# Spreading the gain row over the partitions ahead of the first expert's products instead of between them

## The chip, the cores and the metric

The kernel runs on one core of a Trainium2 chip. What counts is the device time of one execution in microseconds (us). Three runs of the kernel before gave 1275.82, 1276.06 and 1279.53 us; the median is 1276.06 us.

The engines: PE multiplies matrices (PEld is its load of weights, PEq its sequencer), DVE and ACT work on vectors, POOL is GpSimd, SP only issues transfers (SPq is its queue).

## The reference, cut to what matters

One decoder block over 1024 tokens of width 1024. An adaLN-conditioned branch part (windowed attention and a gated MLP) comes first; then a hierarchical mixture of experts: each token takes one group of four, and two of the eight experts in it.

```python
mod = cs @ w_ada[l] + b_ada[l]
sh1, sc1, g1, sh2, sc2, g2 = [m[:, None, :] for m in jnp.split(mod, 6, axis=-1)]
...
h = rms_norm(x, norm2_g[l]) * (1.0 + sc2) + sh2
x = x + g2 * hierarchical_moe(h, w_router_g[l], ..., w_gate[l], w_up[l], w_down[l])
return rms_norm(x, final_g)
```

For each expert the rows of the tokens that chose it go through `(silu(xb @ w_gate) * (xb @ w_up)) @ w_down`; the result is weighted per token and, in this kernel, scaled by the row `g2` (1024 values, one per column) as it is taken out of PSUM. It is this row `g2` that the change is about.

## The kernel before, in words

The first half of the program (attention, gated MLP, output projection) runs from a list `jobs`; the experts run from a second list `jobs2`. A job has a split (a weight piece in fp32 is split into two parts by ACT, L451, and DVE, L452), products on PE, and hooks: functions that are called once the job's products are written down. `Jobs.run` (L88) goes through the list, so the place of a hook is a place in the order of the program. The program's order is not yet the order on the engines: the tile framework's planner gives each engine its queue. It goes through the instructions with the program's order as priority and takes an instruction when its plan holds its operands to be ready, so a later instruction may be queued ahead of an earlier one that still waits. On the chip each engine then works through its queue strictly in that order. Only inside `tc.manual_schedule` is the written order kept.

The row g2 is worked out during the first half (`later_chunk`, L1086) and stored to a DRAM row, `rowd[3]` (L1125). Between the two halves lies the router: for the last two token tiles the logits are multiplied (`r_logit`, L876), ranks within each expert are counted (`r_rank`, L903 to L906), and the list of tokens per first expert is put together by small products (`tab_tok`, L953 to L955, into one PSUM bank for all tiles) and turned into row numbers on DVE (L958, L938, L939, tile `tok_s`). With them POOL gathers the token rows of the first experts by indirect DMA (`gather`, L1425, fetch on L1416), PE transposes them (`x_t`, L1448), ACT takes the transposes out of PSUM (L1449), and the first expert's products can begin (`side`, L1504; 32 rows per expert, so a 128x128 product per quarter). `order_list` (L1688, first product on L1691) sorts the experts on DVE for all later loads.

The experts' weights stream through the pool `big`, 7 buffers of 2 MB; `Ring` issues the next load from the queue of SP (L1391) when a buffer is given back, which is when its last product or split is done. For unit 0 the jobs 0 to 3 are the gate products (16 instructions each), 4 to 7 the up products.

The row g2 reaches the engines thus: SP loads it to partition 0 of tile `G2` (L1832, 4 KB). `spread` (L1822) then multiplies a column of ones by it, once per half of the row, into one fresh PSUM bank each (L1826; the trace shows each call as two matmuls), and ACT copies each half to all 128 partitions of `G2` (L1827). `in_layout` (L1565, copies on L1569) lays the quarters and halves of the row out for experts with 32 and 64 rows (`G2p[4]`, `G2p[2]`), in six copies on POOL. They are first read when an expert's result is taken out (`y_part`, L1571). All of this hangs on job 2 of `jobs2` (L1833): the program writes it between the third and the fourth gate job of the first expert.

Of the kernel before, what the change touches and what calls it, by code (L numbers as in the profile page):

```python
# [101 lines left out]
def block_kernel(ctx: ExitStack, tc: tile.TileContext, x, c, positions, rel_bias, w_ada, b_ada,  # L102
# [6 lines left out]
    PE, DVE, ACT, POOL, SP = nc.tensor, nc.vector, nc.scalar, nc.gpsimd, nc.sync  # L109

    def f(ap):
        return ap.bitcast(F32)
# [8 lines left out]
    def nm(s):  # L121
        uid[0] += 1
        return f"{s}_{uid[0]}"
# [4 lines left out]
    def bank(shape=(512,)):  # L128
        return psum.tile([P] + list(shape), F32, name=nm("ps"), tag="ps")
# [287 lines left out]
    rowd = [dram.tile([1, D], F32, name=f"rowd{i}") for i in range(4)]  # L417
# [32 lines left out]
    def split_to(hi, lo, src):  # L450
        ACT.copy(hi, src)  # L451
        return DVE.tensor_tensor(lo, src, f(hi), op=OP.subtract)  # L452
# [884 lines left out]
    jobs2 = Jobs(2)  # L1337
# [17 lines left out]
    flat = [c for u in units for c in u]  # L1355
# [47 lines left out]
    def parts(i):  # L1403

        return P // rows_of.get(i, P)

    def x_rows(i):

        q = min(parts(i), 2)
        return q, P if i in range(4) else q * rows_of.get(i, P)  # L1410
# [29 lines left out]
    def x_t(i):  # L1440
        xg = XG.pop(i)
        if parts(i) > 1:
            n = x_rows(i)[1]
            xg = xg[0:n, 0:HT].rearrange("t (p j) -> t j p", j=4)
            xt = f(wk.tile([P, 8, P], F32R, name=nm("xTh"), tag="xTh"))[:, 0:4, 0:n]
            ps = bank((4, P))
            for j in range(4):
                PE.transpose(ps[:, j, 0:n], xg[:, j], ident[0:n, 0:n])  # L1448
            ACT.copy(xt, ps[:, :, 0:n])  # L1449
            XT[i] = xt  # L1450
            return
        xg = xg.rearrange("t (h p j) -> t h j p", h=2, j=4)
        hi = wk.tile([P, 8, P], F32R, name=nm("xTh"), tag="xTh")
        lo = wk.tile([P, 8, P], F32R, name=nm("xTl"), tag="xTl")
        for n in range(2):
            ps = bank((4, P))
            for k in range(4):
                PE.transpose(ps[:, k], xg[:, n, k], ident)
            split_to(hi[:, 4 * n:4 * n + 4], lo[:, 4 * n:4 * n + 4], ps)
        XT[i] = (hi, lo)  # L1460
# [104 lines left out]
    def in_layout(dst, src, q):  # L1565

        n, m = P // q, D // q
        for e in range(q):
            POOL.tensor_copy(dst[n * e:n * e + n], src[n * e:n * e + n, m * e:m * e + m])  # L1569
# [66 lines left out]
    G2 = wk.tile([P, D], F32, name="g2r", bufs=1)  # L1636
    G2p = {q: wk.tile([P, D // q], F32, name=f"g2{q}", bufs=1) for q in (2, 4)}
# [43 lines left out]
    def row(n):  # L1681
        return wk.tile([P, 4, n], F32, name=nm("ol"), bufs=1)

    def fl(ap):
        return ap.rearrange("p a b c -> p (a b c)" if len(ap.shape) == 4 else "p a b -> p (a b)")
    key, cap = row(8), row(8)

    def order_list():  # L1688
        b3_ = wk.tile([P, FE], F32, name=nm("sl"), tag="sl")
        pc_ = bank()  # L1690
        PE.matmul(pc_[:, 0:NE], ones_b, cum[:, 0], start=True, stop=True)  # L1691
        top, rank, sel = row(1), row(1), row(4)
        E, S, at, r8 = (b3_[:, 256 + 32 * k:288 + 32 * k].rearrange("p (a b) -> p a b", a=4) for k in range(4))
        b3 = b3_[:, 0:256].rearrange("p (a b c) -> p a b c", a=4, b=8)
        b4 = wk.tile([P, FE], F32, name=nm("sl"), tag="sl")[:, 0:128].rearrange("p (a b c) -> p a b c", a=4, b=8)
        DVE.scalar_tensor_tensor(fl(key), pc_[:, 0:NE], 32.0, fl(tie), op0=OP.mult, op1=OP.add)
        DVE.tensor_reduce(top, key, axis=AX.X, op=OP.max)

        DVE.tensor_tensor(b3, key.unsqueeze(2).to_broadcast([P, 4, 8, 8]), key.unsqueeze(3).to_broadcast([P, 4, 8, 8]),
                          op=OP.is_gt)  # L1700
        DVE.tensor_reduce(r8, b3, axis=AX.X, op=OP.add)

        DVE.tensor_tensor(sel, fl(top).unsqueeze(1).to_broadcast([P, 4, 4]), top.to_broadcast([P, 4, 4]), op=OP.is_gt)
        DVE.tensor_reduce(rank, sel, axis=AX.X, op=OP.add)
        DVE.tensor_tensor(sel, gid.unsqueeze(2).to_broadcast([P, 4, 4]),
                          fl(rank).unsqueeze(1).to_broadcast([P, 4, 4]), op=OP.is_equal)

        DVE.tensor_tensor(b3, place.unsqueeze(1).unsqueeze(3).to_broadcast([P, 4, 8, 8]),
                          r8.unsqueeze(2).to_broadcast([P, 4, 8, 8]), op=OP.is_equal)
        DVE.tensor_tensor(b3, b3, eid.unsqueeze(2).to_broadcast([P, 4, 8, 8]), op=OP.mult)  # L1710
        DVE.tensor_reduce(S, b3, axis=AX.X, op=OP.add)
        DVE.tensor_tensor(b4, sel.unsqueeze(2).to_broadcast([P, 4, 8, 4]),
                          S.rearrange("p g l -> p l g").unsqueeze(1).to_broadcast([P, 4, 8, 4]), op=OP.mult)
        DVE.tensor_reduce(E, b4, axis=AX.X, op=OP.add)
        oi = ord_i[:, 4:NE].rearrange("p (g r) -> p g r", g=4)
        DVE.tensor_copy(oi, E[0:1, :, 0:7])
        DVE.tensor_scalar(cols[:, 4:NE].rearrange("p (g r) -> p g r", g=4), E[:, :, 0:7], 8.0, None, op0=OP.mult)
        DVE.tensor_copy(cols[:, 0:4], iota_c[:, 0:4])
        for j, (g, r) in enumerate(more):
            DVE.tensor_scalar(cols[:, NE + j:NE + j + 1], E[:, g, r:r + 1], 8.0, 1.0, op0=OP.mult, op1=OP.add)  # L1720

        DVE.tensor_tensor(b4, rank.unsqueeze(3).to_broadcast([P, 4, 8, 4]),
                          gid.unsqueeze(1).unsqueeze(1).to_broadcast([P, 4, 8, 4]), op=OP.is_equal)
        DVE.tensor_tensor(b4, b4, room.rearrange("p g r -> p r g").unsqueeze(1).to_broadcast([P, 4, 8, 4]), op=OP.mult)
        DVE.tensor_reduce(at, b4, axis=AX.X, op=OP.add)
        DVE.tensor_tensor(b3, place.unsqueeze(1).unsqueeze(1).to_broadcast([P, 4, 8, 8]),
                          r8.unsqueeze(3).to_broadcast([P, 4, 8, 8]), op=OP.is_equal)
        DVE.tensor_tensor(b3, b3, at.unsqueeze(2).to_broadcast([P, 4, 8, 8]), op=OP.mult)
        DVE.tensor_reduce(cap, b3, axis=AX.X, op=OP.add)
        for g, n in zip(FIRST, FIRST_ROWS):  # L1730
            if n < P:
                DVE.memset(cap[:, g, 0:1], float(n))
# [83 lines left out]
            DVE.tensor_tensor(tm, tok, blk[:, 2 * k], op=OP.mult)  # L1816
            DVE.tensor_tensor(rows_i[:, k], tm, blk[:, 3], op=OP.add)

    order_list()
    x_t(flat[0])  # L1820

    def spread(dst):  # L1822

        for n in range(2):
            sl, ps = slice(512 * n, 512 * n + 512), bank()
            PE.matmul(ps, ones[0:1, :], dst[0:1, sl], start=True, stop=True)  # L1826
            ACT.copy(dst[:, sl], ps)  # L1827
    low = wk.tile([P, 2], F32, name="low", bufs=1)
    R["low"] = low
    DVE.tensor_scalar(low[:, 0:1], prow, 63.5, None, op0=OP.is_lt)  # L1830
    DVE.tensor_scalar(low[:, 1:2], prow, 31.5, None, op0=OP.is_lt)
    SP.dma_start(G2[0:1], rowd[3])  # L1832
    jobs2.hook(2, lambda: (spread(G2), in_layout(G2p[4], G2, 4), in_layout(G2p[2], G2, 2)))  # L1833
    jobs2.hook(3, combine_weights)
    jobs2.hook(4, visits)
    nj = len(jobs2.jobs)
# [79 lines left out]
    jobs2.hook(f_at, f_load)  # L1916
    jobs2.hook(nj - 30, f_gain)
    jobs2.hook(nj - 20, lambda: (spread(F["g"]), in_layout(F[4], F["g"], 4), in_layout(F[2], F["g"], 2)))
    jobs2.hook(nj - 1, final)
    jobs2.run()  # L1920
# [95 lines left out]
def build(inputs):  # L2016
    import concourse.bacc as _bacc

    nc = _bacc.Bacc("TRN2", target_bir_lowering=False, num_devices=1)
    arrays, args = {}, []  # L2020
    for name in _INS:
        a = np.ascontiguousarray(inputs[name])
        arrays[f"in_{name}_dram"] = a
        args.append(nc.dram_tensor(f"in_{name}_dram", a.shape, mybir.dt.from_np(a.dtype), kind="ExternalInput").ap())
    for i, (shape, dtype) in enumerate(_OUTS):
        dt = mybir.dt.from_np(np.dtype(dtype))
        args.append(nc.dram_tensor(f"out_{i}_dram", shape, dt, kind="ExternalOutput").ap())
    with tile.TileContext(nc) as tc:
        block_kernel(tc, *args)
    return nc, arrays  # L2030
# [8 lines left out]
```

## Time and profile before

| | us |
|---|---|
| median of three runs | 1276.06 |
| the profiled execution | 1274.85 |
| its span, first to last instruction | 1273.2 |
| PE busy | 1147.2 (90%) |
| DVE busy | 772.3 (61%) |
| ACT busy | 555.3 (44%) |
| POOL busy | 221.0 (17%) |
| mean DMA rate | 263 GB/s |

All times below are us from the start of the span of that one profiled execution. A row of the timeline gives the start, the length, engine, line, operation, the tile written and those read, shapes, the number of merged instructions, and in brackets how long the engine had been idle and what released it. [...] The first half ends, and the experts begin, at about 690 us.

### The profile page before, as it was taken

Reading aid. Unit: us, or ns where it says so; the run is one execution under the profiler, and the core shown is the slowest. Engines: PE = TensorE matmul, PEld = TensorE weight load, DVE = VectorE, ACT = ScalarE, POOL = GpSimd, SP = SyncE. Lnnn points to the kernel's source line nnn. Section 1 sums busy time; section 2 is a strip of 40 time slices with the busy share of each in tenths; the row PEclk is TensorE's granted clock in tenths of the full one; section 3 lists DMA queues with packets and bytes.
Section 4 is the critical chain, followed back from the end, with each engine's and each line's share of the span. In section 5 each row is a group of like instructions: output and inputs, shape, how many; then the busy total and the mean of one; then the engine's idle time right before and its main releaser. Section 6 shows DMA issues by size and latency. Waiting matters only on the chain. (4 is left out here: it accounts for less than half of the span.)

```text
span 1273.2 us, 18583 instructions
## 1 busy us (share of the span) xinstructions
PE 1147.2 (90%) x6873; PEld 878.1 (69%) x6874; DVE 772.3 (61%) x1698; ACT 555.3 (44%) x970; POOL 221.0 (17%) x325
## 2 busy tenths in 40 slices
PE   5899999999989999899996998998999998899851
PEld 3788887778878988688774665665665656676530
DVE  7668885567767888444497455664425635695015
ACT  4459742335525784233242244543414424673021
POOL 3500010111041000010034211121022121112201
PEclk9999999999989999899995999899999998999975
DMA  9734436547354345523856999999889999999994
GB/s 318 227 103 125 133 114 217 182 158 255 114 185 150 124 133 182 170 85 106 350 200 215 409 401 415 402 381 402 330 299 405 380 324 411 414 360 363 401 409 162
DMA packets 106345, 334.70 MB, mean 263 GB/s; under 512 B 7998, under 2 KB 52158, under 8 KB 81800
## 3 DMA queue, kind: packets, MB, share of 16 engines
q1 hardware_dynamic: 92438, 296.66, 61.6%
q0 software_dynamic: 13712, 36.77, 10.0%
q8 instruction: 55, 0.90, 0.3%
q14 instruction: 42, 0.34, 0.1%
q10 hardware_dynamic: 98, 0.03, 0.0%
HBM read 314.54 MB, written 25.71 MB: 267 GB/s over the span
## 5 line engine op out<-in xcount | busy, mean ns | idle before, releaser
L135 PE MATMUL ps<-big,hi 128*128 128x512 f32 x544 | 220.2, 405 | 9.7 <-ACT hi L451 9.4
L452 DVE TENSOR_TENSOR lo<-big,hi 128x1024 fp32r<-128x1024 f32 x156 | 185.5, 1221 | 67.1 <-ACT hi L451 66.3
L136 PE MATMUL ps<-big,hi 128*128 128x512 f32 x544 | 216.5, 398 | 4.1 <-DVE big L452 4.0
L137 PE MATMUL ps<-big,lo 128*128 128x512 f32 x544 | 215.7, 397 | 0.0
L451 ACT CAST hi<-st 128x512 fp32r<-128x512 f32 x192 | 116.2, 619 | 205.7 <-PE ps L136 117.4
L452 DVE TENSOR_TENSOR lo<-st,hi 128x512 fp32r<-128x512 f32 x192 | 135.3, 715 | 107.1 <-ACT hi L451 106.6
L451 ACT CAST hi<-big 128x1024 fp32r<-128x1024 f32 x156 | 159.4, 1050 | 69.1 <-PE ps L137 68.5
L1504 PE MATMUL ps<-big,xTh 128*32 128x128 f32 (+1 forms) x1792 | 133.4, 337 | 8.0 <-DMA big<-in_w_gate_dram 3.3
L135 PEld LDWEIGHTS ps<-big,hi 128*128 128x128 f32 x544 | 105.0, 193 | 33.4 <-ACT hi L451 11.1
L136 PEld LDWEIGHTS ps<-big,hi 128*128 128x128 f32 x544 | 104.9, 193 | 29.1 <-DVE big L452 5.9
L137 PEld LDWEIGHTS ps<-big,lo 128*128 128x128 f32 x544 | 104.5, 192 | 23.1 <-DVE lo L452 0.9
L1504 PEld LDWEIGHTS ps<-big,xTh 128*32 128x32 f32 (+1 forms) x1792 | 83.3, 126 | 48.7 <-issue 17.1
L136 PE MATMUL ps<-lo,xTh 128*128 128x512 f32 x224 | 94.2, 420 | 12.8 <-DVE lo L452 12.6
L135 PE MATMUL ps<-hi,xTh 128*128 128x512 f32 x224 | 94.2, 421 | 11.2 <-ACT hi L451 11.2
L137 PE MATMUL ps<-hi,xTl 128*128 128x512 f32 x224 | 91.3, 408 | 0.0
L135 PE MATMUL ps<-hi,big 128*128 128x256 f32 (+1 forms) x256 | 88.4, 346 | 0.1
L136 PE MATMUL ps<-lo,big 128*128 128x256 f32 (+1 forms) x256 | 86.8, 339 | 1.1 <-DVE lo L452 1.1
L137 PE MATMUL ps<-hi,big 128*128 128x256 f32 (+1 forms) x256 | 86.5, 338 | 0.0
L1421 POOL DMA_INDIRECT zd<-y,rows_i x30 | 50.8, 1695 | 175.3 <-DVE y L1581 96.1
L1416 POOL DMA_INDIRECT xg<-h2d,rows_i x30 | 36.2, 1207 | 220.9 <-PE ps L1448 101.5
L1504 PE MATMUL ps<-big,aTh 128*32 128x256 f32 (+1 forms) x448 | 64.3, 513 | 5.4 <-DMA big<-in_w_down_dram 5.4
L1577 DVE SCALAR_TENSOR_TENSOR y<-ps,w_sb,g 128x512 f32<-128x512 f32 (+1 forms) x20 | 12.9, 643 | 91.1 <-PE ps L1504 84.0
(382 smaller groups left out, 1865.5 us busy)
## 6 DMA issues: line engine op xcount, KB each, us to landing
big<-in_w_gate_dram SPq DMA_DIRECT2D x32, 2048.0 KB
big<-in_w_up_dram SPq DMA_DIRECT2D x32, 2048.0 KB
big<-in_w_down_dram SPq DMA_DIRECT2D x30, 2048.0 KB
st<-in_w_in_dram SPq DMA_DIRECT2D x26, 1024.0 KB
st<-in_w_ada_dram SPq DMA_DIRECT2D x16, 1024.0 KB
st<-in_w_o_dram SPq DMA_DIRECT2D x10, 1024.0 KB
big<-in_x_dram SPq DMA_DIRECT2D x16, 512.0 KB
bias<-biasd POOLq DMA_DIRECT2D x16, 512.0 KB
```

Source lines behind the costliest of these rows:

```text
L135: PE.matmul(ps, lh, rh, start=start, stop=False)
L136: PE.matmul(ps, lh, rl, start=False, stop=False)
L137: PE.matmul(ps, ll, rh, start=False, stop=stop)
L451: ACT.copy(hi, src)
L452: return DVE.tensor_tensor(lo, src, f(hi), op=OP.subtract)
L1416: return POOL.indirect_dma_start(out=t[0:n, 0:D // q], out_offset=None, in_=in_parts(src, q), in_offset=bass.IndirectOffsetOnAxis(ap=idx[0 ...
L1421: return POOL.indirect_dma_start(out=in_parts(dst, q), out_offset=bass.IndirectOffsetOnAxis(ap=idx, axis=0), in_=t[:, 0:D // q], in_offset ...
L1504: PE.matmul(ps[n * e:n * e + n, 0:m], xt[:, s * i:s * i + n], cols_w, start=start, stop=stop)
L1577: DVE.scalar_tensor_tensor(y, ps[:, 0:D // q], w, G2p[q], op0=OP.mult, op1=OP.mult)
```

## The change

The load of the row, the definition of `spread` and its call move ahead: the load is written before `order_list`, and the two products and two copies directly behind `order_list` and before the first expert's transposes. The six copies of `in_layout` stay at job 2. Nothing is added or removed.

```diff
-    order_list()
-    x_t(flat[0])
-
     def spread(dst):
 
         for n in range(2):
             sl, ps = slice(512 * n, 512 * n + 512), bank()
             PE.matmul(ps, ones[0:1, :], dst[0:1, sl], start=True, stop=True)
             ACT.copy(dst[:, sl], ps)
+    SP.dma_start(G2[0:1], rowd[3])
+    order_list()
+    spread(G2)
+    x_t(flat[0])
+
     low = wk.tile([P, 2], F32, name="low", bufs=1)
...
-    SP.dma_start(G2[0:1], rowd[3])
-    jobs2.hook(2, lambda: (spread(G2), in_layout(G2p[4], G2, 4), in_layout(G2p[2], G2, 2)))
+    jobs2.hook(2, lambda: (in_layout(G2p[4], G2, 4), in_layout(G2p[2], G2, 2)))
```

## Rows read from the trace of the kernel before

**Rows 1.** Timeline of PE from 671 to 705 us.
```profile
671.86 6.89 PE L876 MATMUL ps<-wr,h2T 128*128 128x40 f32 x32
...
682.85 0.18 PE L1691 MATMUL ps<-cum,ones_b 128*128 128x32 bf16 x1 [0.49 <-DVE cum L917]
683.15 0.17 PE L953 MATMUL ps<-tV,tA 128*64 128x8 bf16 x1
...
683.99 0.17 PE L953 MATMUL ps<-tV,tA 128*64 128x8 bf16 x1 [0.46 <-DVE tV L949]
...
684.17 0.19 PE L955 MATMUL ps<-tV,tA 128*64 128x8 bf16 x1
688.83 1.10 PE L1448 MATMUL ps<-ident,xg 128*128 128x128 f32 x4 [4.46 <-DMA xg<-h2d,tok_s]
690.64 2.79 PE L1504 MATMUL ps<-big,xTh 128*32 128x128 f32 x48 [0.72 <-ACT xTh L1449]
693.36 3.78 PE L1826 MATMUL ps<-g2r,ones 1*128 1x512 f32 x4
697.07 1.08 PE L1504 MATMUL ps<-big,xTh 128*32 128x128 f32 x16
...
699.14 3.25 PE L1504 MATMUL ps<-big,xTh 128*32 128x128 f32 x64
```

**Rows 2.** Waits from 1200 us on: us in total, times, longest.
```profile
PE ps L1504 <- DMA big<-in_w_down_dram: 5.4, 2, 2.9
```

**Rows 3.** Stretches: length, then busy time of PE, PEld, DVE, ACT, POOL, granted clock, DMA share, GB/s.
```profile
695.00:700.00 5.00, 5.00 (x40) 2.43 (x42) 0.00 (x0) 3.21 (x5) 2.83 (x7) 0.50 0.19 29
...
701.00:702.00 1.00, 1.00 (x32) 0.93 (x28) 0.00 (x0) 0.00 (x0) 0.03 (x1) 0.60 0.99 418
...
800.00:820.00 20.00, 17.68 (x70) 11.93 (x69) 11.42 (x12) 10.32 (x12) 3.54 (x2) 0.83 1.02 407
...
920.00:940.00 20.00, 20.00 (x119) 14.84 (x120) 8.70 (x11) 4.30 (x7) 2.66 (x2) 1.00 0.76 278
```

**Rows 4.** Timeline of SP's queue from 667 to 703 us.
```profile
667.32 0.37 SPq L1391 DMA_DIRECT2D big<-in_w_gate_dram  x1
667.79 0.27 SPq L1832 DMA_DIRECT2D g2r<-rowd  x1
698.21 0.38 SPq L1391 DMA_DIRECT2D big<-in_w_up_dram  x1
```

**Rows 5.** The product of `left`, hung on job 100: its one execution.
```profile
L1739 PE MATMUL ps<-cum,ones_b x1: 190/190/190, 829.0 to 829.0; 128*128 128x32 bf16 x1
```

**Rows 6.** Timeline of DVE around the lists, and the first expert's product after.
```profile
659.75 1.29 DVE L897 TENSOR_SCALAR lgs<-lg,gm 128x4 f32<-128x4 f32 x1
...
663.24 0.20 DVE L897 TENSOR_SCALAR lgs<-lg,gm 128x4 f32<-128x4 f32 x1
...
702.53 0.29 DVE L1542 TENSOR_TENSOR sl<-sl,ps 128x128 f32<-128x128 f32 x1 [7.85 <-PE ps L1504]
```

**Rows 7.** Timeline of POOL.
```profile
659.70 1.30 POOL L864 TENSOR_TENSOR h<-big,rc 128x512 f32<-128x512 f32 x1
...
685.83 1.11 POOL L1416 DMA_INDIRECT xg<-h2d,tok_s  x1 [4.10 <-DVE jp L1641]
...
696.12 1.51 POOL L1569 COPY g<-g2r 32x256 f32<-32x256 f32 x3 [1.48 <-ACT g2r L1827]
```

**Rows 8.** Timeline of ACT.
```profile
688.02 0.21 ACT L1672 ACTIVATE e<-e 128x8 f32<-128x8 f32 x1 [6.12 <-DVE pg L1673]
...
695.47 0.59 ACT L1827 COPY g2r<-ps 128x512 f32<-128x512 f32 x1 [4.88 <-PE ps L1826]
```

**Rows 9.** PE's timeline from 1202 us: 64 products of the same shape at full clock.
```profile
1202.67 2.04 PE L1504 MATMUL ps<-big,xTh 128*32 128x128 f32 x64
```

**Rows 10.** SP's hardware DMA queue, 674 to 676 and 676 to 678 us: packets, MB, share.
```profile
q1 hardware_dynamic: 56, 0.33, 45.5%
...
q1 hardware_dynamic: 2, 0.00, 0.1%
```

## The prediction

> **What bounds the kernel now.** I read PE's timeline first, because PE is busy for 90% of the span, and asked where around the change it stands still or is slow. Between the router and the experts it does both [rows 1]. The last product of the token lists ends at 684.36 (684.17 + 0.19). PE then waits 4.46 us for the gathered token rows. The transposes run at 688.83, the first 48 gate products from 690.64, the two spread calls from 693.36 to 697.07, and only then the last 16 gate products. So 3.71 us (697.07 - 693.36) of work that no product of the first expert needs stands between its products, right behind a wait that is longer than that work.
>
> Next, does this stretch set the end? The granted clock is 0.50 here [rows 3], so everything on PE takes twice its time. SP issues no weight load from 667.32 to 698.21, which is when the last 16 gate products give the first buffer back [rows 1, 4]; the DMA engines are busy for 0.19 of 695 to 700 [rows 3]. After that they run full for long stretches, but not everywhere: 0.76 in 920 to 940, where PE is busy for all 20 us [rows 3]. The waits show PE waiting for weights only from 1200 on, longest in total for the down weights, 5.4 us [rows 2]. So up to there PE, with DVE and ACT feeding it, sets the pace, and the loads follow from the buffers that it gives back. A shift of PE at 700 goes through to the last drained stretch of the DMA, and from there through the loads to the end. I count a microsecond won or lost ahead of 700 as one at the end.
>
> **The change, part by part.** *Removed from between the products:* both calls, 3.71 us at the low clock: -3.71 [rows 1].
>
> *The row's load.* In SP's queue it already stands directly behind a 2 MB load, at 667.79 against 667.32 [rows 4], and it waits for no step that the move passes. I expect it at the same place: 0. SP's next weight load is 30 us later. Its landing is not shown alone, but SP's hardware queue moved 56 packets from 674 to 676, then 2 in 676 to 678 [rows 10]; I take the row to be in by 678.
>
> *Where the calls go.* The program now has them behind `order_list`, ahead of the transposes, but the planner decides PE's queue. A hint is the product of `left`: its operand, the expert counts, is the one that the product at 682.85 reads, yet it ran at 829.0 [rows 1, 5], though PE stood idle for 4.46 us. Nor were the spread calls drawn into that idle time, though their row was there. Both need a fresh PSUM bank. So I read that a product with a fresh bank is not queued ahead of an earlier one with a fresh bank. Then the calls can come at the earliest behind L1691, whose bank is the last before theirs. That product was itself queued ahead of the lists of the last two tiles, whose bank is older: it runs from 682.85 to 683.03, the lists from 683.15 and 683.99. A planner that fills such a gap puts the first call there. On the chip that call takes half of 3.71, 1.86 us, to 684.89. The two lists follow at 0.37 each (683.99 to 684.36), so the last ends at 685.63, 1.27 late. Everything behind it shifts: the row numbers, the gather (685.83), the transposes. The second call, 1.86 us, then fits into the 4.46 us wait. Bounds of this term: 0 if both calls stand in the wait; 3.13 if both stand ahead of the last list (683.03 + 3.71 + 0.74 - 684.36). I take +1.27, the case that the queue before points to, since L1691 was put into exactly that place.
>
> *The clock.* It is back at 1.00 at about 701.8 (mean 0.60 in 701 to 702, so a fifth of it at full) [rows 3]. That is 4.7 us after the products resume at 697.07, and the spread calls had not brought it back. If uninterrupted products bring it back as fast, it rises 4.7 us behind the start of the gate products instead of 11.2. Then the 64 up products run at full clock: 2.04 us as at 1202.67, instead of 3.25 [rows 1, 9]: -1.2. The other end is 0, if it rises exactly 3.71 earlier relative to those products. I take -1.2, because the calls read one partition only and the clock stayed low through them.
>
> *ACT's two copies* (0.59 each) move from 695.47 into a wait of 6.12 us [rows 8]: 0. Without that cover they would stand ahead of the copy of the transposes and cost at most 1.2.
>
> *POOL's six copies* stay at job 2 in the program but can run as soon as the row is spread: two groups of three, 1.51 us each [rows 7]. They leave 696 to 699, where DVE does nothing, for the time of DVE's sorting. That DVE work ends long before the first expert's product needs the engine (7.85 us idle [rows 6]); stretched by all 3.0 us it stays hidden even in a start that comes 3.6 earlier. Only copies queued ahead of the first gather, in POOL's wait of 4.10 us, can hurt: between 0 and 1.51 (one group). I take 0, because the copies have lower priority than the gather and are ready at nearly the same time; the other end is kept for the range.
>
> On that, a row: a DVE instruction on 4 values took 1.29 us at 659.75, when POOL had a product of two tiles running from 659.70 for 1.30, against 0.20 at 663.24 [rows 6, 7]. [...]
>
> *Sum:* -3.71 + 1.27 - 1.2 = -3.64. The profiled execution took 1274.85 (span 1273.2, 1.65 around it), so 1271.2; it lay 1.21 under the median of the runs, and on the median the forecast is 1276.06 - 3.64 = 1272.4.
>
> **Rivals.** *1. Both calls stand in the wait for the gather.* The wait (4.46) holds them (3.71). For: the program has them right there. Against: L1691's place shows that gaps ahead of the last lists are filled. Result: -3.71 - 1.2 = -4.9: 1271.2.
>
> *2. Both calls ahead of the last list.* For: if the plan holds the lists to be ready later than the chip does. Against: two lists only 0.84 us apart leave little room for a second call. Result: -3.71 + 3.13 - 1.2 = -1.8: 1274.3.
>
> *3. The change does not do what it says.* If the planner holds the row to land late, behind the 2 MB load, both calls come again with or behind the first products. For: before, they were not used to fill the wait; a late row explains that as well as the banks do (but not L1739's place). Result: 0: 1276.1.
>
> *4. Slower: the calls are queued ahead of the last logits.* If fresh banks bind less than I read and the plan holds the row to be there early, the calls stand ahead of the products at 671.86. PE keeps its order, and the row lands only in 676 to 678 [rows 10]. PE would wait 4.1 to 6.1 us and then run 3.71, and all of that lies ahead of logits, lists and gather: +7.8 to +9.8, less 3.71 and 1.2: +2.9 to +4.9, middle 1280.0. It decides when the first call stands ahead of L876 in PE's order. Against: the same two places that speak for the banks.
>
> **How the numbers follow.** Forecast 0.34, rival 1 0.28, rival 2 0.14, rival 3 0.13, rival 4 0.11. Each scatters by about 1.5 us: a drop of the clock as in 800 to 820 (mean 0.83, so a third of 20 us at half rate [rows 3]) comes or stays away with small shifts, and the runs before lie 3.7 apart. Forecast and rival 1 alone give 1270 to 1274. The range reaches down to 1268.8 for rival 1 with more from the clock, and up to 1278.3, which takes in rival 3 and about a quarter of rival 4; little more than 1 in 10 lies above, under 1 in 10 below. A measurement of this kernel tells about 0.3%, 3.8 us, from no change, so the line lies at 1272.2, just under the forecast. Faster: most of rival 1 (0.22), nearly half of the forecast (0.16), a little of rival 2 (0.02): 0.40. Slower: two thirds of rival 4 and a rest: 0.10. Within: 0.50.
>
> **What would show it.** Right: the calls (L1826) start between 683 and 688 with one or both outside the products; the gate products run unbroken; SP issues its first weight load of the experts 2.4 to 3.7 us before 698.21; the clock is back 4 to 6 us behind the first gate product. The lists' ends against 684.36 and the gather against 685.83 show the term of +1.27. The copies on POOL stand behind the first gather or not. Wrong: calls behind 690; a wait of L1826 for its DMA; a gather later than 689.5 (685.83 + 3.71), which eats up all that was removed; or the win at 700 gone again by 1200.

## The result: slower, and the profile after

The changed kernel took 1284.54 us (median of 20 runs, 1276.6 to 1288.18) against 1276.39 of the kernel before (20 runs, 1272.28 to 1282.36): a ratio of 1.0055 with a 95% interval of 1.0039 to 1.007, some 7 us more. Here and below a ratio leaves out the few slow runs and is taken over the single runs, so it is not quite the quotient of the medians, which lie 8.15 us apart here. The prediction was 1272.4, with 0.10 for slower; the range, up to 1278.3, did not hold the time.

The profiled execution took 1288.18 us. The page of the changed kernel, span, busy times and clock in 40 slices:

```profile
span 1286.5 us, 18583 instructions
...
PE 1158.4 (90%) x6873; PEld 884.5 (69%) x6874; DVE 773.2 (60%) x1698; ACT 554.8 (43%) x970; POOL 220.4 (17%) x325
...
PEclk9899998999999999899996698999999998999975
```

The counts of instructions are those of before; only PE is busier (1147.2 before). PE's timeline after the change answers to [rows 1]:

```profile
689.15 0.18 PE L1691 MATMUL ps<-cum,ones_b 128*128 128x32 bf16 x1 [0.49 <-DVE cum L917]
...
690.60 3.78 PE L1823 MATMUL ps<-g2r,ones 1*128 1x512 f32 x4
694.97 1.13 PE L1448 MATMUL ps<-ident,xg 128*128 128x128 f32 x4 [0.59 <-DMA xg<-h2d,tok_s]
696.82 3.64 PE L1504 MATMUL ps<-big,xTh 128*32 128x128 f32 x64 [0.72 <-ACT xTh L1449]
...
701.27 2.05 PE L1504 MATMUL ps<-big,xTh 128*32 128x128 f32 x64
705.71 0.66 PE L1780 MATMUL ps<-y 128*128 128x68 f32 x4 [2.39 <-POOL y L1778]
...
720.75 0.70 PE L1801 MATMUL ps<-y,jp 128*128 128x68 f32 x2
...
723.88 5.07 PE L1504 MATMUL ps<-big,xTh 128*32 128x128 f32 x72
728.98 0.33 PE L1552 MATMUL ps<-ident,sl 128*128 128x128 f32 x1
```

The same view of the kernel before, further down than [rows 1] go:

```profile
702.32 0.66 PE L1780 MATMUL ps<-y 128*128 128x68 f32 x4
...
711.93 0.44 PE L1801 MATMUL ps<-y,jp 128*128 128x68 f32 x2
...
714.20 3.06 PE L1504 MATMUL ps<-big,xTh 128*32 128x128 f32 x72
717.19 0.33 PE L1552 MATMUL ps<-ident,sl 128*128 128x128 f32 x1
```

I count from L1691, since everything ahead of it runs in the same order in both kernels and its start scatters from profile to profile (682.85 here before, 689.15 after). What was moved does what it should: both calls (L1823 now) fill the wait for the gather, of which 0.59 us is left, and the up products end 14.17 us behind L1691 (701.27 + 2.05 - 689.15) instead of 19.54 (699.14 + 3.25 - 682.85): 5.37 us won. Then PE waits 2.39 us for POOL at the first product of the tables (`table`, L1780: small products that put together the lists of rows and weights for the later experts, between the first experts' products). About 2 us later the granted clock is 0.50 and a group of four L1780 takes 1.12 us instead of 0.66, and the last L1552 above starts 39.83 behind L1691 instead of 34.34. So 5.37 us are won and 10.86 lost behind them. The stretches of the changed kernel (columns as in [rows 3]) show how:

```profile
705.00:707.00 2.00, 1.29 (x21) 1.01 (x22) 0.52 (x2) 0.00 (x0) 1.76 (x6) 1.00 0.57 115
707.00:710.00 3.00, 3.00 (x37) 2.38 (x41) 1.08 (x5) 0.27 (x1) 1.50 (x5) 0.64 0.98 410
710.00:720.00 10.00, 10.00 (x76) 6.07 (x72) 1.93 (x8) 0.28 (x1) 2.22 (x8) 0.50 1.02 424
720.00:725.00 5.00, 4.02 (x40) 2.67 (x36) 2.85 (x20) 0.96 (x2) 0.00 (x0) 0.50 1.00 400
```

and of the kernel before:

```profile
710.00:720.00 10.00, 8.92 (x126) 5.92 (x125) 4.75 (x24) 3.03 (x5) 3.00 (x4) 1.00 1.02 423
```

Behind the wait the granted clock drops from 1.00 to 0.50, at about 707.8 by the mean of 0.64 in 707 to 710, and stays there past 725 (0.50 in 725 to 728), though PE is busy for all of 710 to 720. The kernel before has 1.00 in the same work (702.3 to 717.5). The loss adds up: 2.39 of waiting; 15.04 us instead of 9.61 from the first L1780 to the first L1801 (+5.43); 8.23 instead of 5.26 from there to L1552 (+2.97): 10.79 of 10.86.

Why POOL is late stands in its timeline, after:

```profile
694.13 1.05 POOL L1416 DMA_INDIRECT xg<-h2d,tok_s  x1 [0.30 <-issue]
695.19 0.41 POOL L1569 COPY g<-g2r 32x256 f32<-32x256 f32 x1
698.74 1.06 POOL L1569 COPY g<-g2r 32x256 f32<-32x256 f32 x2 [3.15 <-DMA xg<-h2d,tok_s]
699.96 1.13 POOL L1416 DMA_INDIRECT xg<-h2d,tok_s  x1 [0.16 <-issue]
703.52 1.50 POOL L1569 COPY g<-g2r 32x256 f32<-32x256 f32 x3 [2.44 <-DMA xg<-h2d,tok_s]
705.11 0.30 POOL L1777 TENSOR_TENSOR y<-y,wts 128x68 f32<-128x68 f32 x1
705.37 0.29 POOL L1778 TENSOR_TENSOR y<-y,pay 128x68 f32<-128x68 f32 x1
```

and before:

```profile
690.20 1.18 POOL L1416 DMA_INDIRECT xg<-h2d,tok_s  x1 [1.32 <-PE ps L1448]
693.46 0.41 POOL L1777 TENSOR_TENSOR y<-y,wts 128x68 f32<-128x68 f32 x1 [2.08 <-DVE y L932]
693.83 0.29 POOL L1778 TENSOR_TENSOR y<-y,pay 128x68 f32<-128x68 f32 x1
...
697.82 1.52 POOL L1569 COPY g<-g2r 32x256 f32<-32x256 f32 x3 [0.20 <-ACT g2r L1827]
```

L1777 and L1778 make the operands of the table products (tile `y`, one pair per table). Before, the first pair was done at 694.12, 8.2 us ahead of its product at 702.32, and the six copies came behind it. After, the row is spread earlier, so the planner queues all six ahead of the pair, although `in_layout` is still written at job 2. Twice the copies then stand still for the landing of a gather (3.15 and 2.44 us), and the pair behind them is done only at 705.66. Its operand from DVE had been there since 700.33:

```profile
700.11 0.22 DVE L932 TENSOR_TENSOR y<-cols,rc 128x68 f32<-128x68 int32 x1
```

Without the copies the pair would have been done soon after that, ahead of the 703.32 at which the up products end.

### The profile page after: what moved, and what is told of

It reads as the page before. It is cut to its first block, busy times and chain, and to the rows that moved or that the text cites. A ratio compares the mean times of both kernels' runs of the same rounds, so it can differ in the third digit from the quotient of the medians.

```text
span 1286.5 us, 18583 instructions
## 1 busy us (share of the span) xinstructions
PE 1158.4 (90%) x6873; PEld 884.5 (69%) x6874; DVE 773.2 (60%) x1698; ACT 554.8 (43%) x970; POOL 220.4 (17%) x325
## 4 chain that ended last, share of the span: by engine, by line
PE 55%; DVE 8%; DMA 8%; issue 2%; ACT 2%; POOL 1%; POOLq 0%; ACTq 0%; DVEq 0%; SPq 0%
PE ps L136 12%; PE ps L135 12%; PE ps L1504 12%; PE ps L137 12%; DVE lo L452 3%; DMA big<-zd 2%; DMA big<-in_w_gate_dram 2%; DMA st<-in_w_ada_dram 1%; ACT hi L451 1%; PE ps L1458 1%; PE ps L876 1%; PE ps L1559 1%; PE ps L1448 1%; DMA xg<-h2d,tok_s 1%; PE ps L1780 1%
## 5 line engine op out<-in xcount | busy, mean ns | idle before, releaser
L1504 PE MATMUL ps<-big,xTh 128*32 128x128 f32 (+1 forms) x1792 | 134.9, 341 | 7.6 <-DMA big<-in_w_gate_dram 3.3
L1504 PEld LDWEIGHTS ps<-big,xTh 128*32 128x32 f32 (+1 forms) x1792 | 84.1, 127 | 47.6 <-issue 16.4
L1504 PE MATMUL ps<-big,aTh 128*32 128x256 f32 (+1 forms) x448 | 66.4, 535 | 5.3 <-DMA big<-in_w_down_dram 5.3
L1577 DVE SCALAR_TENSOR_TENSOR y<-ps,w_sb,g 128x512 f32<-128x512 f32 (+1 forms) x20 | 12.9, 644 | 92.8 <-PE ps L1504 85.7
```

Source lines behind the costliest of these rows:

```text
L1504: PE.matmul(ps[n * e:n * e + n, 0:m], xt[:, s * i:s * i + n], cols_w, start=start, stop=stop)
L1577: DVE.scalar_tensor_tensor(y, ps[:, 0:D // q], w, G2p[q], op0=OP.mult, op1=OP.mult)
```

## The experiments

My theory behind the result: the copies' new place on POOL delays the first table's operands, PE's wait for them exceeds what the calls had cost, and the lower clock behind it costs most. The rivals: the row's spread itself, in its new place, does the harm (for instance by the clock or ACT); or the wait alone counts and the clock would have fallen anyway. Each kernel is one edit of the changed kernel, if not said otherwise, and each ratio is against the kernel before on the same chip.

**The copies behind the second pair.** All else as in the changed kernel.

```diff
-    jobs2.hook(2, lambda: (in_layout(G2p[4], G2, 4), in_layout(G2p[2], G2, 2)))
+    def layouts():
+        with tc.issue_after(R["V", 1].ins):   # behind L1778 of the second table
+            in_layout(G2p[4], G2, 4)
+            in_layout(G2p[2], G2, 2)
+    jobs2.hook(8, layouts)
```

> The changed kernel, but the six copies of the row's quarters and halves are queued on POOL behind the products for token tables 0 and 1 (L1777, L1778) instead of ahead of them. Theory A (POOL's queue): in the changed kernel these copies, now ready early, stand ahead of the tables' operands, PE waits 2.4 us for them at table 0, and its clock falls to 0.50 for some 20 us, which costs about 11 us against the 5 us that were won at the first products. Then this kernel keeps the win and loses the cost: PE does not wait for POOL at L1780, the clock stays at 1.00 after the first up products, and the time is 4 to 6 us under the kernel before (1270 to 1272.5). Theory B (the loss lies elsewhere: ahead of the experts, where the profiled execution of the changed kernel was already 6.1 us late, or in the code's place in memory): the time stays 5 to 8 us over the kernel before.

Measured: 1272.69 us, ratio 0.9971 (0.9954 to 0.9989). PE has no wait at the first table:

```profile
692.70 2.03 PE L1504 MATMUL ps<-big,xTh 128*32 128x128 f32 x64
694.66 0.66 PE L1780 MATMUL ps<-y 128*128 128x68 f32 x4
```

and on POOL the pair stands first, the six copies run without a stop:

```profile
691.41 0.41 POOL L1777 TENSOR_TENSOR y<-y,wts 128x68 f32<-128x68 f32 x1 [2.08 <-DVE y L932]
...
692.54 3.06 POOL L1569 COPY g<-g2r 32x256 f32<-32x256 f32 x6
```

The spread in its new place is a gain; the whole loss hangs on the copies' place. (The third table's product still waits 0.55 us for POOL in this kernel; the clock is 1.00 in 695 to 730.)

**The copies ahead of the third gather.** They stay ahead of the pair, but the third gather now waits for the last of them, so that none of them can wait for that gather to land:

```diff
-                gather(flat[i + 2])
+                with tc.issue_after(R["lay"].ins) if i == 0 else ExitStack():   # R["lay"]: the last copy
+                    gather(flat[i + 2])
```

> The changed kernel with all six copies queued on POOL ahead of the third gather (L1416), so that the second three need not wait for that gather to land. It asks what in POOL's queue delays the operands of table 0: the copies themselves (3.0 us) or the wait for the gather's landing (2.44 us in the changed kernel) in front of the second three. If the landing: the operands come within 0.5 us of PE's wish or sooner, PE's clock stays at 1.00 behind the first up products, and the time is 2 to 5 us under the kernel before. If the copies' own length is enough: PE waits 1 us or more at table 0, and the time stays over the kernel before when the clock falls, by 3 to 7 us.

Measured: 1275.22 us, ratio 0.9976 (0.995 to 1.0003).

```profile
696.03 3.11 POOL L1569 COPY g<-g2r 32x256 f32<-32x256 f32 x5 [3.34 <-DMA xg<-h2d,tok_s]
...
700.53 0.30 POOL L1778 TENSOR_TENSOR y<-y,wts 128x68 f32<-128x68 f32 x1
```

```profile
701.14 0.66 PE L1781 MATMUL ps<-y 128*128 128x68 f32 x4 [0.85 <-POOL y L1779]
```

One of the two waits for a gather is left, PE waits 0.85 us instead of 2.39, and the granted clock is 1.00 in 700 to 715. So the second wait for a landing makes the difference between a wait that was followed by the low clock and one that was not. What is left, the copies and the first landing, still brings the pair 0.85 us too late; the expectation had allowed 0.5.

**The wait filled.** POOL's queue as in the changed kernel; PE gets twelve products that nothing reads.

```diff
+        if t == 0 and n == NT:
+            busy = bank()
+            with tc.issue_after(R["side"].ins):   # the last product so far
+                for _ in range(12):
+                    PE.matmul(busy, ones_b, wide2, start=True, stop=True)   # wide2: 128x512, bf16
```

> The changed kernel with 12 products of 128x512 in bf16, whose result nobody reads, put behind the first up products, where PE waits for table 0. POOL's queue stays as in the changed kernel. It tells the price of the wait from the price of the clock. Theory A1 (the wait costs mostly through the clock): the clock stays at 1.00 from 705 to 725, the L1504 products of the next experts take 32 ns apart instead of 64, and the time is 6 to 9 us under the changed kernel, 0 to 3 us under the kernel before. Theory A2 (the clock falls there by its own phase, whatever PE does; the wait costs only itself): the clock falls as before and the time is that of the changed kernel, within 2 us. Theory B: the time of the changed kernel too.

Measured: 1273.92 us, ratio 0.9987 (0.997 to 1.0004).

```profile
699.63 2.76 PE L1782 MATMUL ps<-wide,ones_b 128*128 128x512 bf16 x11
...
703.35 0.66 PE L1787 MATMUL ps<-y 128*128 128x68 f32 x4 [0.96 <-POOL y L1785]
```

```profile
710.00:720.00 10.00, 8.83 (x125) 5.88 (x127) 6.66 (x27) 3.79 (x5) 3.05 (x5) 1.00 1.02 423
```

(The trace has a record of 11 of the 12 products.) POOL's queue is as late as before, yet the clock is 1.00 in 700 to 720 and the loss against the kernel before is gone. So the rival that the clock falls anyway is out: with the wait filled down to 0.96 us it does not.

**The opposite on the kernel before: POOL held up there.** The spread stays between the products; POOL clears an unused tile twelve times between the copies and the first pair.

```diff
+        if t == 0 and n == NT:
+            with tc.issue_after(R["lay"].ins):   # R["lay"]: the last copy
+                for _ in range(12):
+                    last = POOL.memset(idle, 0.0)   # 128x256
+        gate = tc.issue_after(last.ins) if t == 0 and n == NT else ExitStack()
-        POOL.tensor_tensor(V[:, :, 0], ...)
-        POOL.tensor_tensor(V[:, :, 1], ...)
+        with gate:
+            POOL.tensor_tensor(V[:, :, 0], ...)
+            POOL.tensor_tensor(V[:, :, 1], ...)
```

> The kernel before, unchanged but for 12 memsets of 128x256 that nobody reads, queued on POOL between the six copies and the operands of table 0; so those operands come about 3 us after PE wants them (705.3 against 702.3). Theory A1: PE waits some 3 us at the first L1780, its clock falls to 0.50, and the time rises by 8 to 12 us although nothing of the change is in this kernel. Theory A2: it rises by 3 us. Theory B: 0 to 3 us.

Measured: 1286.3 us, ratio 1.0078 (1.0053 to 1.0103), the changed kernel's loss without its change.

```profile
701.91 4.01 POOL L1781 MEMSET idle<- 128x256 f32 x11
705.98 0.30 POOL L1784 TENSOR_TENSOR y<-y,wts 128x68 f32<-128x68 f32 x1
```

```profile
706.58 1.12 PE L1787 MATMUL ps<-y 128*128 128x68 f32 x4 [3.62 <-POOL y L1785]
...
712.89 1.12 PE L1787 MATMUL ps<-y 128*128 128x68 f32 x4
```

PE waits 3.62 us and the groups of four products take 1.12 instead of 0.66 (the second 0.96): the clock, 0.50 in 706 to 725. Delay of POOL's pair is enough to cause a loss of this size without the change.

**No spread at all: the row by DMA.** Seven transfers write the row to all partitions and into both layouts; the calls, ACT's copies and POOL's six are gone.

```diff
-    SP.dma_start(G2[0:1], rowd[3])
+    SP.dma_start(G2, bcast(rowd[3], D))
+    for q in (4, 2):
+        n, m = P // q, D // q
+        for e in range(q):
+            SP.dma_start(G2p[q][n * e:n * e + n], bass.AP(...))   # m values of the row to n partitions
     order_list()
-    spread(G2)
```

> The changed kernel with the row spread by DMA: SP loads it to all 128 partitions, and its quarters and halves to their places, in seven transfers at the place of the one load (0.9 MB in all); the two products, the two ACT copies and the six POOL copies are gone. Theory A: nothing stands between or ahead of the first products, and POOL's queue has no copies ahead of the tables: 4 to 6 us under the kernel before, like the kernel with the copies behind, unless the transfers, which run when the DMA engines are full, push the last loads ahead of the gather back (at most 0.9 MB at 400 GB/s, 2.3 us). Theory B: 5 to 8 us over the kernel before.

Measured: 1271.63 us, ratio 0.9974 (0.9952 to 0.9996). Beside the kernel with the copies behind (0.9971) it shows that, once the copies are out of the way, the spread in the wait for the gather costs nothing that can be told.

**The same with that wait filled.** Ten of the same unread products behind the last token list, ahead of the transposes.

```diff
     order_list()
+    busy = bank()
+    with tc.issue_after(R["tabmm"].ins):   # the last product of the token lists
+        for _ in range(10):
+            PE.matmul(busy, ones_b, wide2, start=True, stop=True)
     x_t(flat[0])
```

> The kernel with the row spread by DMA, and 10 products of 128x512 in bf16, whose result nobody reads, in PE's wait of 4.4 us for the first gather, where the changed kernel has the two calls of the spread. It asks why the clock did not come back during those calls: my reason was that they read one partition only. If so, full products bring the clock back in or just behind the wait; the 64 gate products then take 2.05 us instead of 3.64, and the time is 1 to 3 us under the kernel with the row by DMA (5 to 7 us under the kernel before). If any product counts alike, or none in so short a wait, the gate products stay at 3.6 us and the time within 1 us of the kernel with the row by DMA.

Measured: 1271.51 us, ratio 0.9969 (0.995 to 0.9988).

```profile
682.86 3.96 PE L1837 MATMUL ps<-wide,ones_b 128*128 128x512 bf16 x10
...
688.81 2.05 PE L1506 MATMUL ps<-big,xTh 128*32 128x128 f32 x64 [0.72 <-ACT xTh L1451]
...
692.27 2.53 PE L1506 MATMUL ps<-big,xTh 128*32 128x128 f32 x64
...
706.67 4.61 PE L1506 MATMUL ps<-big,xTh 128*32 128x128 f32 x72
```

The gate products take 2.05 us instead of 3.64. The changed kernel filled the same wait for 3.78 us with products of one row, and its gate products still ran at a clock of 0.50 (mean of 696.8 to 700.46). But the gain is partly given back: the up products take 2.53 (2.05 after), and the 72 products at 706 take 4.61 (3.06 before). Those 72 stand behind a wait of 0.98 us for DVE, as in the kernel before. In the kernel with the row by DMA they take 4.24, behind the same wait. At 1.00 they took 3.06 (before), at 0.50 5.07 (after), so I estimate that in these two kernels most of them ran at 0.50; why, behind the wait of 0.98 us, is not shown. Against the kernel with the row by DMA the time shows no difference; the 1 to 3 us that were expected are not to be seen.

**And POOL's clears moved behind the tables' first pairs.** On top of the last one, the four clears of tile `z` (L1657 before) leave the time of DVE's ranks.

```diff
-        POOL.memset(Z[i], 0.0)
...
+    def z_clear():
+        with tc.issue_after(R["gather"].ins):   # the last gather written so far
+            for i in ends:
+                POOL.memset(Z[i], 0.0)
+    jobs2.hook(20, z_clear)
```

> The kernel with the row by DMA and the filled wait, and besides the four memsets of the tiles Z (L1657), which POOL runs beside the router's DVE steps, put behind the operands of table 1. In the kernel before a DVE cast of two values took 1.11 us beside the first of these memsets instead of 0.16, and PE waited 1.88 us for the step behind it. If POOL's memset holds DVE up, that cast is back at 0.16 and the list of the last tile ends about 0.9 us sooner behind the last logits; the time is 1 us under the kernel without this, 6 to 8 us under the kernel before. If not, the cast and the time stay.

Measured: 1271.84 us, ratio 0.9956 (0.9935 to 0.9976), the lowest ratio of all, but not to be told from 0.9969. In the kernel without this edit, a cast on DVE that ran beside the clears:

```profile
680.20 1.30 POOL L1659 MEMSET z<- 128x512 f32 x4
```

```profile
680.56 0.97 DVE L915 CAST si<-sf 128x2 int32<-128x2 f32 x1
```

and the same cast with the clears away:

```profile
687.61 0.16 DVE L915 CAST si<-sf 128x2 int32<-128x2 f32 x1
```

From L1693 (the earlier L1691) to the first gather it is 3.78 us with them (684.39 - 680.61) and 2.99 without (690.65 - 687.66). So the clears cost about 0.8 us there; the measured time is too coarse to show that. In the kernel before, the held-up cast (1.11 us at 680.64) stands ahead of L1691, so that from L1691 to the first gather it is 2.98 us there too.

**The changed kernel once more**, unchanged, for a second profile:

> The changed kernel once more, for a second trace. Theory A: PE waits again 2 to 3 us for POOL at table 0 and the clock falls right behind it and stays at 0.50 for 15 to 25 us. If the fall was a matter of phase, the second trace has the wait without it. The stretch ahead of the experts should differ from the first trace by microseconds, since no instruction of it differs and other kernels had their product on L1691 between 680.8 and 689.2.

Measured: 1282.14 us, one run.

```profile
700.90 0.66 PE L1780 MATMUL ps<-y 128*128 128x68 f32 x4 [3.20 <-POOL y L1778]
...
703.01 1.08 PE L1504 MATMUL ps<-big,xTh 128*32 128x128 f32 x16
```

The wait is there again, 3.20 us, and 2.1 us behind its end 16 products of L1504 take 1.08 us (703.01), where before they took 0.66.

**All profiles in one table.** Start of L1691 (or its line in the edited kernel), time from there to the last L1552 shown above (the second of its kind in the window), rest of the span, and the wait at the first table (a dash: none shown):

| kernel | start | to L1552 | rest | wait | ratio of times |
|---|---|---|---|---|---|
| before | 682.85 | 34.34 | 556.0 | - | 1 |
| changed | 689.15 | 39.83 | 557.5 | 2.39 | 1.0055 |
| changed again | 683.32 | 41.26 | 555.9 | 3.20 | one run |
| copies behind | 680.80 | 29.40 | 556.8 | - | 0.9971 |
| copies ahead of the third gather | 686.24 | 29.82 | 556.4 | 0.85 | 0.9976 |
| wait filled | 685.68 | 33.03 | 553.0 | 0.96 | 0.9987 |
| before, POOL late | 683.54 | 47.23 | 553.1 | 3.62 | 1.0078 |
| row by DMA | 686.95 | 31.68 | 556.1 | - | 0.9974 |
| same, wait filled | 680.61 | 31.43 | 556.0 | - | 0.9969 |
| same, clears late | 687.66 | 27.54 | 557.1 | - | 0.9956 |

The middle column goes with the ratios, though not one to one: 39.83 and 41.26 against 34.34 is +5.5 and +6.9, where the measured ratio makes about +7 of 1276; 29.40 is -4.9, where 0.9971 makes -3.7; 47.23 is +12.9, where 1.0078 makes +10 and the rest is 2.9 shorter. In the two kernels with 31.68 and 31.43 the cast that the clears hold up falls behind L1691 (the first gather comes 3.96 and 3.78 us behind it, 2.98 or 2.99 in the others), so 1.0 and 0.8 us of these numbers stand ahead of L1691 in most of the others. The start scatters by 8 us over the profiles with no order that I can see in it, by 5.8 for the changed kernel alone, which is why a single pair of spans (+13.3 here) does not give the size of the change.

## Why the prediction was wrong

*The step that failed is "POOL's six copies": "I take 0".* I asked what the copies would do to DVE's sort and whether they would stand ahead of the first gather, and priced the latter at 1.51 at most. I did not ask what is queued behind them on POOL. That is the pair of operands for the first table, due only a few microseconds later, and it is due earlier than before, since the products ahead of the table end 5.37 us sooner. The cost measured is 2.39 us of wait and, through the clock, 8.4 us more (5.43 + 2.97). The prediction named "the win at 700 gone again by 1200" as what would make it wrong; it was gone 11 us behind the end of the up products, at the sixth table (714.55). The end that was "kept for the range" is that of another place: no bound I wrote covers this. Nor did the fourth rival, slower by calls ahead of the last logits; nothing of that happened.

*The copies "stay at job 2 in the program".* That says nothing of POOL's queue. I had written myself that the planner takes an instruction when its operands are ready; moving the spread moved the readiness of all that hangs on it. The rows showed the copies at 696.12, released by ACT's copy of the row [rows 7], and the trace has the two pairs ahead of them: readiness had held them there, not the hook.

*-3.71 and -1.2:* right. The calls are gone from between the products, and the up products take 2.05 instead of 3.25. The rest of the 5.37 is small: 0.12 at the start of the gate products, 0.34 in them and in the transposes behind them.

*+1.27, a call ahead of the last two lists:* wrong. Both calls stand behind the lists, as in the first rival, whose win (4.9) is close to the 5.37 of the stretch. Why L1691 was put ahead of the lists and the calls were not is not shown. Counted from L1691, the first call starts 1.45 us behind it, where the prediction's 683 to 688 is 0.15 to 5.15 behind.

*The clock "is back 4 to 6 us behind the first gate product":* right (696.82 to at latest 701.27; 0.50 in 696.8 to 700.46, 0.99 in 701 to 702). That it could be lost again 6.5 us later (707.8), behind a wait that did not exist before, was not weighed.

*ACT's copies, 0:* right; they ran at 694.44, ahead of the transposes' copy at 696.18, and PE's wait for that copy is 0.72 as before.

*SP's first load, "2.4 to 3.7 us before 698.21":* wrong, without effect on the time. I had it follow the gate products [rows 4]. But SP first reads the order of the experts, one value after the other, and nothing of that stands in the rows I had read. The last step of each such read, up to the load (x: how many; then the shortest, middle and longest in ns, and the first and last start), before:

```profile
L1362 SPq SEQ_ASSERT  x14: 18/18/18, 689.8 to 697.6; - x14
```

and after:

```profile
L1362 SPq SEQ_ASSERT  x15: 18/18/18, 696.4 to 704.7; - x15
```

That is about 0.6 us each. Before, the last one ended 0.6 us ahead of the load, which could then follow the products. After, with one more read queued and the products done earlier, the reads end last: the load leaves at 704.79, 4.3 us behind the gate products, and the DMA is at a share of 0.18 in 700 to 705. The rest of the span is the same (556 to 557.5), so this costs nothing that shows.

*DVE's work beside POOL's copies, "stretched by all 3.0 us it stays hidden":* right; DVE was idle for 1.96 us before its first step on the first expert's products (L1542, 703.45). The cast at L1716 took 0.42 instead of 0.16 while the first copy ran (695.19 to 695.60):

```profile
695.21 0.42 DVE L1716 CAST ord_i<-sl 1x28 int32<-1x28 f32 x1
```

The product at L1765 took 0.56 instead of 0.16 beside the next two (699.26). So beside copies these two steps took 0.26 and 0.40 us longer, off the path. Beside POOL's clears a cast took 0.97 instead of 0.16. By what means they took longer no run shows.

*Open:* why copies wait for a gather's landing, twice. The copies read and write nothing of the gathered rows; what tile, buffer or semaphore causes it was not tried. Open too is why the low clock lasted for some 20 us behind the wait, when it was back within 4.45 us of the first gate product in the same kernel, and why the start of L1691 scatters by 8 us.

## What to carry to other kernels

When an operation is moved ahead, list everything that becomes ready with it, and for each of those the engine's queue: what stands behind it now, and when that is due in the new, shorter schedule. A wait of 2.39 us on PE cost 10.8 here with the low clock behind it, so I would price a new wait of that length, as an estimate from these runs, with the products behind it at the times they took at 0.50 (1.12 us for four of a table instead of 0.66). If a dependent step is not urgent, tie it behind what is urgent on its engine: here that one edit turned +0.55% into -0.3%.

## What the runs showed of the hardware

- Behind waits of 2.39 and 3.62 us ahead of the first table's product the granted clock was 0.50 (708 to 728 in the changed kernel, 706 to 725 in the kernel before with POOL late); behind the wait of 3.20 us the tables' groups of four took 1.12 us, as at 0.50. Behind those of 0.85 and 0.96 us at the same place it was 1.00 in 700 to 715. That is no bound: further on, behind the same wait of 0.98 us, the clock was 1.00 in the kernel before, where 72 products took 3.06 us, and in the two kernels with the row by DMA and the clears in place they took 4.24 and 4.61. In the changed kernel the low clock behind the 2.39 us held until past 725, through 10 us in which PE was busy without a gap, with products of 68 columns and of quarters.
- At 0.50 against 1.00 groups of the same products took 3.64 and 2.05 us (64 gate and 64 up products), 5.07 and 3.06 (72 products), 1.12 and 0.66 (four of a table): 1.7 to 1.8 times, where the prediction has "everything on PE takes twice its time".
- Products of one row (4 in 3.78 us) ran at 0.50, and the clock was still 0.50 in the transposes and gate products behind them, to 700.46; ten full bf16 products (3.96 us) in the same wait were followed by gate products in 2.05 us instead of 3.64.
- Beside POOL's four clears (1.30 us together) a DVE cast took 0.97 us, with the clears away 0.16.
